# A two-layer retention and latent-attention trunk: the later modulation summed along rows, loaded early, and a reordered first unit

## The chip, the cores and the metric

The kernel runs on one core of one Trainium2 chip. The metric is device time in microseconds (us) for one call; lower is better. The engines are named as in the profile: PE (TensorE, matmuls; PEld are its weight loads), DVE (VectorE), ACT (ScalarE), POOL (GpSimd) and SP (SyncE, which only issues DMA transfers here). Each takes its instructions in order.

## What is computed

One sequence of 512 tokens, width 2048, float32, two layers. Each layer is normalised, shifted, scaled and gated by a conditioning vector `c`:

```python
c_act = jax.nn.silu(c)
for i in range(DEPTH):
    mod = (c_act @ ada_w[i] + ada_b[i])[:, None, :]          # 2048 -> 3 * 2048
    shift, scale, gate = jnp.split(mod, 3, axis=-1)
    h = rmsnorm(x, norm_g[i]) * (1.0 + scale) + shift
    y = retention_branch(...) if i == 0 else mla_branch(...)
    x = x + gate * y
return rmsnorm(x, final_norm_g)
```

Layer 1 (`i == 0`) is multi-scale retention with 8 heads: an input projection to queries and keys (256 each per head), values and a gate (512 each per head), chunked retention, a group norm, a SiLU gate and an output projection. Layer 2 is latent attention with 16 heads, again with a SiLU gate. The modulation is a vector times a 2048 x 6144 matrix per layer, some 100 MB of weights in all that are used once.

## The kernel before

Every large product is made in three matmuls (`mm3`), of a high and a low half of each operand, so every weight tile that arrives is cast on ACT (high half) and subtracted on DVE (low half) before PE reads it. PSUM has four banks under the tag `acc` and four under `aux`. SBUF tiles are taken from tagged pools: a tag has a fixed number of buffers, and a new tile waits until the oldest holder of a buffer is done, with a store's landing if a store reads it. Those that matter here are `tmp` (6 buffers of 128 x 512), `whi` and `wlo` (3 each, halves of weights), `raw` (3, weights as they arrive), and in the pool `lp`, which lives while layer 1 is projected, `st` (2), `bw` (2) and `bm` (2).

The program goes in stages. (1) The first unit and the seven that follow it compute head 0's projections (value, gate, query-key) for two contraction tiles of 128 at a time, while x is normalised and transposed (`transpose`) and while the first layer's shift and scale arrive from `ada_t`, a copy of the weights with outputs on rows. `load_mod` loads 128 outputs x 2048, `sum_mod` multiplies them on DVE with c, which stands on every partition (`c_all`), and sums along the row in the same instruction (L358); `make_first` makes one contraction tile of h from it (hT), its low half on DVE. `swap` saves partial sums from four banks on ACT and puts back others. (2) Heads 1 to 7: for heads 1 to 5 eight query-key steps of 24 matmuls, then for every head sixteen steps for values and gate together (`heads_steps`, `seven_steps`), the second eight of 18 matmuls. At a head's end `finish` evacuates the banks x_ (values) and s_ (gate) on ACT through `keep_rows`, adds y_ to the tiles m4 and m5 on DVE, and stores all eight row blocks to DRAM on POOL's queue. m4 and m5 are `tmp` tiles that were filled from banks some steps earlier. (3) The query-key steps of heads 6 and 7, and the output projection of layer 1 beside the retention of all heads. (4) Layer 2, with its gate projections (`g2_steps`), the attention and the last projection.

What is left of the modulation, first-layer gate and all of layer 2, is spread over stages 2 to 4 in eight pieces of 1024 outputs (`later_modulation`). A piece has 16 loads of 512 KB from `ada_w`, with the contraction on partitions. DVE multiplies each by one column of silu(c) per partition and adds it into `am` (L893, L895); two steps later PE sums `am` over partitions with a column of ones into eight columns of an `aux` bank (`sum_modulation`, L907), and `use_modulation` adds the biases. `rows` of a step says how many loads are issued at the end of the step before it; their adds come in that step, behind the preparation of the next step's weights. Four pieces are loaded in stage 2 (one load a step in the query-key steps of heads 2 to 5, and in second halves), two in stage 3 (`light`), two in stage 4 at two loads a step. `behind` and `queued` fix the order on an engine: what they enclose is put behind the last instruction so far on the engines named.

`keep_rows` takes its staging tile from `st`, or from another function if it is given one (`own`): the gate's tiles and every second query-key tile come from `tmp`.

Of the kernel before, what the change touches and what calls it, by code (L numbers as in the profile page):

```python
# [16 lines left out]
P = 128  # L17
# [32 lines left out]
def hybrid_trunk_kernel(  # L50
# [39 lines left out]
    x1_d = dram.tile([D, T], F32, name="x1_d")  # L90
    sg2_d = dram.tile([D, T], F32, name="sg2_d")
# [120 lines left out]
    cact = base.tile([P, KD], F32, name="cact")  # L212
    ACT.dma_start(cact, c.rearrange("o (p k) -> p (o k)", p=P))
    ACT.dma_start(rt, rot_c)
    ACT.activation(cact, cact, AF.Silu)
# [84 lines left out]
    ada0 = ada_w[0].rearrange("(p k) n -> p k n", p=P)  # L300
    ada1 = ada_w[1].rearrange("(p k) n -> p k n", p=P)

# [38 lines left out]
    def load_mod(kt, s):  # L341

        aw = l0p.tile([P, D], F32, tag="aw", bufs=4, name=f"aw_{kt}_{s}")
        n = 2 if kt == 0 else 1
        for j in range(n):
            cols = slice(j * D // n, (j + 1) * D // n)
            nc.sync.dma_start(aw[:, cols], ada_t[s * D + kt * P : s * D + (kt + 1) * P, cols])
        return aw
# [114 lines left out]

    ss = [small(f"x_ss_{t}", 2) for t in range(NT)]
# [26 lines left out]
    queued(diagonal, NT - 1)  # L491
    low_v = queued(prepares["v", 0])
# [15 lines left out]
    for kt in range(6):  # L508
        queued(queued(transpose, kt))
    def load_unit(u):  # L510
# [8 lines left out]
    late = {}  # L519

    def prepare_ahead(u, first=None):
# [5 lines left out]
        if first is not None:  # L527
            queued(first)
# [6 lines left out]
        late[u] = queued(prepares[there, u])  # L535
# [3 lines left out]
    def prepare_behind(u):  # L539

        low = queued(make_first, 2 * u + 1)
        queued(late[u])
        return low

# [7 lines left out]
    lows = [queued(prepares[kind, 0]) for kind in ("g", "qk")]  # L552
    for low in lows:
        queued(low)
# [99 lines left out]
    class Step:  # L654
# [3 lines left out]
        def __init__(self, load=None, prepare=None, multiply=None, follow=None, rows=0, sums=None, banks_free=False):  # L658
            self.units = [(load, prepare)] if load else []
            self.multiply, self.follow = multiply, follow or (lambda: None)  # L660
            self.rows, self.sums, self.banks_free = rows, sums, banks_free
# [62 lines left out]
    def seven_steps(h, block, form, raw_tile, part_tiles, finish, rows, free):  # L724
# [16 lines left out]
        def step(second, u):  # L741
# [67 lines left out]
            return Step(load, prepare, multiply, follow, rows=rows(second, u), banks_free=free(second, u))  # L809
# [3 lines left out]
    def heads_steps(h):  # L813
# [3 lines left out]
        def finish(x_, s_, y_, m4, m5):  # L817
            for b in range(2):
                keep_rows(x_[b], v_d, h * T + b * P, f"v{h}_st{b}")
            for b in range(2):  # L820
                keep_rows(s_[b], g_d, h * T + b * P, f"g{h}_st{b}", AF.Silu, tmp)
# [11 lines left out]
            lambda second, u: int(second and (u % 2 == 1 or (h > 4 and u > 0))),  # L833
            lambda second, u: second and h == RH - 1 and 2 < u < 7,
# [18 lines left out]
    def in_turn(i):  # L853
        return None if i % 2 else tmp

# [5 lines left out]
    for h in range(1, RH):  # L861
        if h < 6:
# [1110 lines left out]
```

## Time and profile before

| | |
|---|---|
| median of 3 runs | 2210.42 us (2210.02 to 2212.81) |
| the profiled execution's own time | 2211.04 us |
| its span, first to last instruction | 2209.2 us, granted clock 0.996 |
| PE busy | 2171.6 us, 98% |
| DVE busy | 1569.7 us, 71% |
| ACT busy | 995.4 us, 45% |
| POOL busy | 98.4 us, 4% |
| DMA | 437.13 MB, mean 198 GB/s |

A row of a timeline is start, duration, engine, line, operation, output tile <- input tiles, shapes and count, and in brackets how long the engine had been idle and what released it. A row of waits is the waiting instruction, what released it, the total, how often, and the longest. A row of groups ends in busy time, mean nanoseconds of one, and idle time before. Matmuls overlap, so their starts and not their durations show the rate.

### The profile page before, as it was taken

The page shows a single profiled execution, that of the slowest core. Times are in us where ns is not written, and L with a number is a line of the kernel's source. Part 1 is how long each engine was busy: PE and PEld are TensorE (multiplying, and loading weights), DVE is VectorE, ACT ScalarE, POOL GpSimd, SP SyncE. Part 2 cuts the span into 40 slices and gives each one's busy share as a digit, 9 for nine tenths or more (in the row PEclk, how much of TensorE's full clock was granted, in tenths as well). Part 3 has the DMA queues.
Part 4 walks back from the last instruction along what each step waited for, and adds up shares of the span by engine and source line. Part 5 has one row for each costly group of instructions (what it writes and reads, how often), then busy time and mean ns, then how long its engine had stood idle before and what let it go on. Part 6 is the DMA issues. An engine that isn't in the chain of part 4 may idle for free.

```text
span 2209.2 us, 28064 instructions
## 1 busy us (share of the span) xinstructions
PE 2171.6 (98%) x10404; PEld 1818.8 (82%) x10404; DVE 1569.7 (71%) x2355; ACT 995.4 (45%) x1496; POOL 98.4 (4%) x175
## 2 busy tenths in 40 slices
PE   7999999999999999999999999999999999999997
PEld 5887888888888888888888888898888888888886
DVE  7878867677676789666776767667967677776545
ACT  5664434334343454434344445345444355554443
POOL 0010000000000000000000000010001000000000
PEclk9999999999999999999999999999999999999998
DMA  9964685867677778564646565453557623225332
GB/s 384 347 247 153 223 283 189 285 196 257 229 229 251 240 244 293 188 205 147 212 167 214 167 205 181 138 177 96 172 195 285 239 77 96 82 91 195 121 122 92
DMA packets 208207, 437.13 MB, mean 198 GB/s; under 512 B 19364, under 2 KB 64436, under 8 KB 204228
## 3 DMA queue, kind: packets, MB, share of 16 engines
q1 hardware_dynamic: 195744, 396.16, 54.1%
q0 software_dynamic: 11888, 38.90, 4.5%
q8 instruction: 81, 1.33, 0.3%
q14 instruction: 60, 0.47, 0.1%
q10 hardware_dynamic: 434, 0.28, 0.1%
HBM read 392.28 MB, written 42.99 MB: 197 GB/s over the span
## 4 chain that ended last, share of the span: by engine, by line
PE 79%; DVE 9%; ACT 5%; issue 5%; DMA 2%; POOL 0%; POOLq 0%; DVEq 0%; ACTq 0%
PE o L1192 13%; PE qk L162 4%; PE qk L160 4%; PE qk L161 4%; PE o L1892 4%; PE x L733 2%; PE x L734 2%; PE y L734 2%; PE y L732 2%; PE y L733 2%; PE x L732 2%; PE s L734 2%; PE s L733 2%; PE s L732 2%; PE g L160 2%
## 5 line engine op out<-in xcount | busy, mean ns | idle before, releaser
L1192 PE MATMUL o<-o_h,o_whi 128*128 128x512 f32 (+1 forms) x496 | 193.1, 389 | 0.0
L1192 PE MATMUL o<-o_l,o_whi 128*128 128x512 f32 (+1 forms) x496 | 192.0, 387 | 0.0
L1192 PE MATMUL o<-o_h,o_wlo 128*128 128x512 f32 (+1 forms) x496 | 191.9, 387 | 0.0
L162 PE MATMUL qk<-hT,qk_l 128*128 128x512 f32 x448 | 174.8, 390 | 0.5 <-DVE qk_l L135 0.5
L160 PE MATMUL qk<-hT,qk_h 128*128 128x512 f32 x448 | 174.8, 390 | 0.0
L161 PE MATMUL qk<-hT,qk_h 128*128 128x512 f32 x448 | 174.3, 389 | 0.0
L895 DVE SCALAR_TENSOR_TENSOR mod_am<-mod_aw,cact,mod_am 128x1024 f32<-128x1024 f32 x120 | 153.6, 1280 | 15.4 <-DMA mod_aw<-in_ada_w_dram 14.9
L135 DVE TENSOR_TENSOR o_wlo<-o_r,o_whi 128x1024 fp32r<-128x1024 f32 x61 | 74.6, 1223 | 87.2 <-ACT o_whi L134 87.2
L135 DVE TENSOR_TENSOR qk_l<-qk_r,qk_h 128x1024 fp32r<-128x1024 f32 x56 | 68.1, 1223 | 66.6 <-ACT qk_h L134 66.6
L1192 PEld LDWEIGHTS o<-o_h,o_wlo 128*128 128x128 f32 x496 | 93.6, 189 | 19.0
L1192 PEld LDWEIGHTS o<-o_l,o_whi 128*128 128x128 f32 x496 | 93.7, 189 | 18.4
L1192 PEld LDWEIGHTS o<-o_h,o_whi 128*128 128x128 f32 x496 | 93.5, 189 | 18.4
L162 PEld LDWEIGHTS qk<-hT,qk_l 128*128 128x128 f32 x448 | 84.1, 188 | 19.5 <-DVE qk_l L135 2.0
L161 PEld LDWEIGHTS qk<-hT,qk_h 128*128 128x128 f32 x448 | 84.1, 188 | 17.3
L160 PEld LDWEIGHTS qk<-hT,qk_h 128*128 128x128 f32 x448 | 84.1, 188 | 17.2
L134 ACT CAST qk_h<-qk_r 128x1024 fp32r<-128x1024 f32 x56 | 57.8, 1048 | 88.8 <-PE qk L161 68.5
L160 PE MATMUL g<-h,g_h 128*128 128x512 f32 x232 | 90.7, 391 | 0.3 <-ACT g_h L134 0.3
L161 PE MATMUL g<-h,g_h 128*128 128x512 f32 x232 | 90.3, 389 | 0.0
L162 PE MATMUL g<-h,g_l 128*128 128x512 f32 x232 | 89.8, 389 | 0.0
L358 DVE SCALAR_TENSOR_TENSOR aw<-aw,c_all 128x2048 f32<-128x2048 f32 (+1 forms) x34 | 73.3, 2160 | 2.5 <-DMA aw<-in_ada_t_dram 2.5
L134 ACT CAST o_whi<-o_r 128x1024 fp32r<-128x1024 f32 x61 | 63.5, 1052 | 24.1 <-PE o L1192 11.4
L135 DVE TENSOR_TENSOR o_w_lo<-o_w_raw,o_w_hi 128x1024 fp32r<-128x1024 f32 x32 | 39.0, 1220 | 34.6 <-ACT o_w_hi L134 34.5
(1249 smaller groups left out, 5983.6 us busy)
## 6 DMA issues: line engine op xcount, KB each, us to landing
mod_aw<-in_ada_w_dram SPq DMA_DIRECT2D x128, 512.0 KB, 5.4
o_r<-in_ret_w_out_dram SPq DMA_DIRECT2D x64, 512.0 KB, 4.5
aw<-in_ada_t_dram SPq DMA_DIRECT2D x30, 1024.0 KB, 8.8
qk_r<-in_ret_w_in_dram SPq DMA_DIRECT2D x112, 256.0 KB, 4.0
g_r<-in_mla_w_in_dram SPq DMA_DIRECT2D x32, 512.0 KB, 3.9
o_w_raw<-in_mla_w_out_dram SPq DMA_DIRECT2D x32, 512.0 KB, 3.9
qk_d<-qk_st POOLq DMA_DIRECT2D x32, 256.0 KB, 3.4
qk_r<-qk_d SPq DMA_DIRECT2D x32, 256.0 KB, 6.4
```

Of the source, the lines that this page charges most:

```text
L134: ACT.copy(hi, src)
L135: DVE.tensor_sub(lo, src, hi.bitcast(F32))
L160: PE.matmul(o, lhs[0], rhs[0], start=first and not seeded, stop=False, skip_group_check=seeded)
L161: PE.matmul(o, lhs[0], rhs[1], start=False, stop=False, skip_group_check=seeded)
L162: return PE.matmul(o, lhs[1], rhs[0], start=False, stop=last, skip_group_check=seeded)
L358: DVE.scalar_tensor_tensor(out=aw[:, cols], in0=aw[:, cols], scalar=1.0, in1=c_all[:, cols], op0=ALU.mult, op1=ALU.mult, accum_out=col[:, ...
L732: PE.matmul(banks[b], a[0], w[0], start=first, stop=False, skip_group_check=True)
L733: PE.matmul(banks[b], a[0], w[1], start=False, stop=False, skip_group_check=True)
L734: PE.matmul(banks[b], a[1], w[0], start=False, stop=True, skip_group_check=True)
L895: DVE.scalar_tensor_tensor(out=am, in0=aw, scalar=ck, in1=am, op0=ALU.mult, op1=ALU.add)
L1192: PE.matmul(o, w[i][:, ki, c0 + b * P : c0 + (b + 1) * P], a[j], start=first and i + j == 0, stop=last and i == 1, skip_group_check=True,)
L1892: PE.matmul(banks2[b][:, cols], w[0][i][:, 0, b * P : (b + 1) * P], o2_moving(w, u, cols)[j], start=u + i + j == 0, stop=u == KD - 1 and i ...
```

## The change

The eight later pieces are loaded from `ada_t`, which now holds both layers whole: a load is 128 outputs x 1024 contraction elements, again 512 KB, and there are again 16 a piece. DVE multiplies it by half of c on all partitions and sums along the row in one instruction. `am`, the ones matmuls on PE, `ripe`, `summed` and the markers `banks_free` go. silu(c) is written to DRAM once (`keep_c`) and read back onto all partitions, in `lp` and again in layer 2. `bw` in `lp` has three buffers; `bm` and `st` are not used there any more, and every `keep_rows` stages in `tmp`. Six of the eight pieces are loaded in stage 2, with two loads a step in the query-key steps of heads 2 to 5; the output projection of layer 1 has none; the last two stay in layer 2. In the first unit the copies of the transposes 4 and 5 come later, 6 and 7 come right after the first query-key products, the order of preparations on ACT and DVE is written out, and v is multiplied at the end for both contraction tiles with `bank_products`, after its first tile has been multiplied at the start as before.

Left out below: declarations, the parameters `free` and `banks_free` wherever they are passed, `light`, and the layout of `ada_t` on the input side.

```diff
     bias1 = l0p.tile([P, KD], F32, name="bias1")
+    def keep_c():
+        POOL.dma_start(c_d, c_all[0:1, :])
+
     ss = [small(f"x_ss_{t}", 2) for t in range(NT)]
     norm = [None] * NT
...
         if t > 0:
             queued(diagonal, t - 1)
     queued(diagonal, NT - 1)
+    keep_c()
     low_v = queued(prepares["v", 0])
     queued(lambda: DVE.tensor_scalar(out=bias1, in0=bias_c[0][:, KD:], scalar1=1.0, scalar2=None, op0=ALU.add))
...
             )
         return lambda: ACT.copy(xT[kt // 2][:, kt % 2, :], ps)
-    for kt in range(6):
+    for kt in range(4):
         queued(queued(transpose, kt))
+    copies = [queued(transpose, kt) for kt in (4, 5)]
+
     def load_unit(u):
         here, there = ("qk", "v") if u % 2 == 0 else ("v", "qk")
         load_first(here, u)
...
-    late = {}
-
-    def prepare_ahead(u, first=None):
+    late_there = {}
+
+    def prepare_ahead(u, first):
...
-        if first is not None:
-            queued(first)
+        queued(first)
...
     queued(sum_mod, 1, 0)
     queued(low)
     lows = [queued(prepares[kind, 0]) for kind in ("g", "qk")]
+    for copy in copies:
+        queued(copy)
     for low in lows:
         queued(low)
     queued(sum_mod, 1, 1)
...
     queued(swap, "v", "qk")
     low = queued(make_first, 1)
     queued(products, "qk", 0)
-    prepare_ahead(1, low)
+    for kt in (6, 7):
+        queued(queued(transpose, kt))
+    queued(sum_mod, 2, 0)
+    queued(low)
+    low = queued(prepares["v", 1])
+    queued(sum_mod, 2, 1)
+    queued(low)
     queued(products, "qk", 1)
-    queued(queued(transpose, 6))
     queued(products, "g", 1)
     queued(swap, "qk", "v")
-    low = prepare_behind(1)
-    queued(queued(transpose, 7))
-    queued(products, "v", 1)
+    low = queued(make_first, 2)
+    for s in range(2):
+        queued(sum_mod, 3, s)
+    queued(low)
+    low = queued(prepares["g", 1])
+    low3 = queued(make_first, 3)
+    queued(low)
+    late = queued(prepares["qk", 1])
+    queued(bank_products, "v", 0)
+    queued(late)
+    low = low3
     for u in range(1, NU):
         here, there = ("qk", "v") if u % 2 == 0 else ("v", "qk")
...
     lp = tc.tile_pool(name="lp", bufs=1)
     lpp = lp.__enter__()
-    def keep_rows(ps, dst_d, r0, name, func=AF.Identity, own=None):
-
-        st = lpp.tile([P, T], F32, tag="st", bufs=2, name=name) if own is None else own(name)
+    def keep_rows(ps, dst_d, r0, name, func=AF.Identity):
+
+        st = tmp(name)
         ACT.activation(st, ps, func)
         POOL.dma_start(dst_d[r0 : r0 + P, :], st)
...
             for b in range(2):
                 keep_rows(x_[b], v_d, h * T + b * P, f"v{h}_st{b}")
             for b in range(2):
-                keep_rows(s_[b], g_d, h * T + b * P, f"g{h}_st{b}", AF.Silu, tmp)
+                keep_rows(s_[b], g_d, h * T + b * P, f"g{h}_st{b}", AF.Silu)
             for b in range(2):
                 r0 = h * T + (2 + b) * P
                 DVE.tensor_add(m4[b], m4[b], y_[b])
...
         return seven_steps(
             h, lambda kt, j: wvg[kt * P : (kt + 1) * P, j, h * T : (h + 1) * T],
             lambda n, u, b: form(hT, sums1, n, u, b), *turns1, finish,
-            lambda second, u: int(second and (u % 2 == 1 or (h > 4 and u > 0))),
-            lambda second, u: second and h == RH - 1 and 2 < u < 7,
+            lambda second, u: int(second and u in ((1, 2, 3, 4, 5, 7) if h > 4 else (1, 3, 5, 7))),
         )
     sums1, sums2 = {}, {}
...
             steps += plain_steps(
                 8, 2, qk_parts_of(h), 512, f"qk{h}", acc, 4,
                 lambda w, ki, kt, b: w_block(w, ki, b), lambda w, ki, kt, b: act_row(hT[kt]),
-                lambda b, ps, h=h: keep_rows(ps, qk_d, (4 * h + b) * P, f"qk{h}_st{b}", own=in_turn(b)),
-                rows=lambda u, h=h: int(h > 1),
+                lambda b, ps, h=h: keep_rows(ps, qk_d, (4 * h + b) * P, f"qk{h}_st{b}"),
+                rows=lambda u, h=h: 2 * int(h > 1),
                 sums=lambda u, h=h: {0: 2, 1: 3, 3: 4, 4: 5, 6: 6, 7: 7}.get(u) if h == 1 else None,
-                banks_free=lambda u: u < 5,
             )
         steps += heads_steps(h)
-
-    ripe, summed, clock = [], [], [0]
-
-    def later_modulation(pool, pieces, tags=("bm", (("bw", 2),))):
-
+    def later_modulation(pieces, silu_c, buffers):
+
+        n = 0
         for i, sect, part in pieces:
             name = f"mod_{i}_{sect}_{part}"
-            c0 = sect * D + part * 1024
-            am = pool.tile([P, 2, T], F32, tag=tags[0], bufs=2, name=f"{name}_am")
-            for k in range(KD):
-                tag, bufs = tags[1][k % len(tags[1])]
-                aw = pool.tile([P, 2, T], F32, tag=tag, bufs=bufs, name=f"{name}_aw{k}")
-                nc.sync.dma_start(
-                    aw, (ada0, ada1)[i][:, k : k + 1, c0 : c0 + 1024].rearrange("p k (a n) -> p (k a) n", a=2)
-                )
-
-                def add(aw=aw, am=am, k=k, what=(name, i, sect, part, am)):
-                    ck = cact[:, k : k + 1]
-                    if k == 0:
-                        DVE.tensor_scalar(out=am, in0=aw, scalar1=ck, scalar2=None, op0=ALU.mult)
-                    else:
-                        DVE.scalar_tensor_tensor(out=am, in0=aw, scalar=ck, in1=am, op0=ALU.mult, op1=ALU.add)
-                    if k == KD - 1:
-                        ripe.append((clock[0], what))
-
-                yield add
-
-    def sum_modulation(age=2):
-
-        while ripe and clock[0] - ripe[0][0] >= age:
-            name, i, sect, part, am = ripe.pop(0)[1]
-            ps = aux(f"{name}_ps")
+            mc = base.tile([P, 2, 8], F32, tag="mod_c", bufs=2, name=f"{name}_c")
             for b in range(8):
-                PE.matmul(ps[:, b : b + 1], am[:, b // 4, b % 4 * P : (b % 4 + 1) * P], crow, start=True, stop=True)
-            summed.append((i, sect, part, ps[:, 0:8]))
-
-    def use_modulation():
-        while summed:
-            i, sect, part, mc = summed.pop(0)
-            if sect == 2:
-                cols = slice(part * 8, part * 8 + 8)
-                DVE.tensor_add(gate_c[i][:, cols], mc, gate_bias[i][:, cols])
-            else:
-                modulate(i, mc if sect == 0 else None, mc if sect == 1 else None, part * 8, 8)
+                for j in range(2):
+                    pool, tag, bufs = buffers[n % len(buffers)]
+                    n += 1
+                    aw = pool.tile([P, 2, T], F32, tag=tag, bufs=bufs, name=f"{name}_{b}{j}")
+                    r0 = sect * D + (8 * part + b) * P
+                    nc.sync.dma_start(
+                        aw, ada_t[i, r0 : r0 + P, j * 1024 : (j + 1) * 1024].rearrange("p (a n) -> p a n", a=2)
+                    )
+
+                    def add(aw=aw, j=j, b=b, mc=mc, i=i, sect=sect, part=part):
+                        DVE.scalar_tensor_tensor(
+                            out=aw, in0=aw, scalar=1.0, in1=silu_c[j], op0=ALU.mult, op1=ALU.mult,
+                            accum_out=mc[:, j, b : b + 1],
+                        )
+                        if b == 7 and j == 1:
+                            use_modulation(i, sect, part, mc)
+
+                    yield add
+
+    def use_modulation(i, sect, part, mc):
+        both = small(f"mod_{i}_{sect}_{part}_s", 8)
+        DVE.tensor_add(both, mc[:, 0, :], mc[:, 1, :])
+        if sect == 2:
+            cols = slice(part * 8, part * 8 + 8)
+            DVE.tensor_add(gate_c[i][:, cols], both, gate_bias[i][:, cols])
+        else:
+            modulate(i, both if sect == 0 else None, both if sect == 1 else None, part * 8, 8)
     def token_sums(ps, ss, n0, n):
...
             lambda w, ki, kt, b: w_block(w, ki, b), lambda w, ki, kt, b: act_row(hT[kt]),
             lambda b, ps, h=h: keep_rows(
                 ps, qk_d, (4 * h + b) * P, f"qk{h}_st{b}",
-                own=tmp,
             ),
         )
     n_p = len(steps)
-    light(block, ())
     steps += block
     heads = [retention(0, k4), retention(1, k4, odd)]
...
         for r, after in zip(cols, [*cols[1:], None]):
             block += round_steps(n, r, go_on(n, r, after))
         heads += [retention(2 * n + 2 + i, big) for i in range(2)]
-        light(block, (0, 2, 3, 4, 6, 7, 10, 11, 12, 14, 15))
         steps += block
...
         g23[i + 1].beside["form"].append(lambda n=n: latent_scale(n))
         g23[2 + 2 * i].beside["multiply"].append(lambda n=n: latent_transposes(n))
         g23[3 + 2 * i].beside["form"].append(lambda n=n, g_c=g_c: latent_parts(n, g_c))
-    for step in g23[8:]:
-        step.banks_free = True
     steps += g23
     def all_rows():
-        yield from later_modulation(lpp, [(i, s_, n) for i, s_ in ((0, 2), (1, 0)) for n in range(2)])
-        while "l1" not in pools:
-            yield None
-        yield from later_modulation(pools["l1"], [(1, 1, n) for n in range(2)], ("odd1", (("odd0", 2),)))
+        c_all = lpp.tile([P, 2, 2, T], F32, name="c_all_p")
+        nc.sync.dma_start(c_all.rearrange("p a b n -> p (a b n)"), c_d.rearrange("o n -> (o n)").partition_broadcast(P))
+        pieces = [(i, s_, n) for i, s_ in ((0, 2), (1, 0), (1, 1)) for n in range(2)]
+        yield from later_modulation(pieces, [c_all[:, j] for j in range(2)], [(lpp, "bw", 3)])
         while "l2" not in pools:
             yield None
-        yield from later_modulation(pools["l2"], [(1, 2, n) for n in range(2)], ("bm", (("bw", 2), ("pt", 4))))
+        silu_c = [k4b(f"c_{j}", F32) for j in range(2)]
+        for j, half in enumerate(silu_c):
+            nc.sync.dma_start(
+                half.rearrange("p a n -> p (a n)"),
+                c_d[0:1, j * 1024 : (j + 1) * 1024].rearrange("o n -> (o n)").partition_broadcast(P),
+            )
+        yield from later_modulation(
+            [(1, 2, n) for n in range(2)], silu_c, [(pools["l2"], "bw", 2), (pools["l2"], "pt", 4), (pools["l2"], "pt", 4)]
+        )
     later = all_rows()
     loads = [load for step in steps for load, _ in step.units]
...
     n_loaded = 3
     n_prepared = prepare_for(0)
     for b in range(4):
-        queued(keep_rows, qk0[b], qk_d, b * P, f"qk0_st{b}", AF.Identity, in_turn(b))
+        queued(keep_rows, qk0[b], qk_d, b * P, f"qk0_st{b}")
     for b in range(3):
-        queued(keep_rows, g0[b], g_d, b * P, f"g0_st{b}", AF.Silu, tmp)
+        queued(keep_rows, g0[b], g_d, b * P, f"g0_st{b}", AF.Silu)
     for i, step in enumerate(steps):
-        clock[0] = i
         if i == n_p:
             lp.__exit__(None, None, None)
             l1 = tc.tile_pool(name="l1", bufs=1)
             pools["l1"] = l1.__enter__()
         if i == n_l2:
-            assert not ripe and not summed
             l1.__exit__(None, None, None)
             l2 = tc.tile_pool(name="l2", bufs=1)
             pools["l2"] = l2.__enter__()
...
                 load()
         n_prepared += prepare_for(i + 1)
         with behind(V_, A_):
-            use_modulation()
             for form_ in step.beside["form"]:
                 form_()
-        with behind(T_):
-            if step.banks_free:
-                sum_modulation()
         with behind(T_):
             step.multiply()
         with behind(T_):
```

More of the change, by code (lines that the diff above doesn't have):

```diff
@@ L534, in prepare_ahead @@
         low = queued(prepares["g", u])
-        late[u] = queued(prepares[there, u])
+        late_there[u] = queued(prepares[there, u])
         queued(low)
@@ L541, in prepare_behind @@
         low = queued(make_first, 2 * u + 1)
-        queued(late[u])
+        queued(late_there[u])
         return low
@@ L722, in turns, with seven_steps @@
         return raw_tile, part_tiles
-    def seven_steps(h, block, form, raw_tile, part_tiles, finish, rows, free):
+    def seven_steps(h, block, form, raw_tile, part_tiles, finish, rows):
         x_, s_, y_, z_, m1, m4, m5 = ([None] * 2 for _ in range(7))
@@ L807, in follow @@
                     finish(x_, s_, y_, m4, m5)
-            return Step(load, prepare, multiply, follow, rows=rows(second, u), banks_free=free(second, u))
+            return Step(load, prepare, multiply, follow, rows=rows(second, u))
         return [step(second, u) for second in (False, True) for u in range(KD // 2)]
@@ L1099, in place @@
                 block[first + i].beside[kind].append(fn)
-    def light(block, which):
-        for i in which:
-            block[i].rows = 1
-        for i in (2, 3):
-            block[i].banks_free = True
     block = []
```

21 lines of the change are left out of this document (6 added, 15 removed).

## The prediction

> **What bounds the kernel now.** The page comes first.
>
> ```profile
> span 2209.2 us, 28064 instructions
> PE 2171.6 (98%) x10404; PEld 1818.8 (82%) x10404; DVE 1569.7 (71%) x2355; ACT 995.4 (45%) x1496; POOL 98.4 (4%) x175
> PE   7999999999999999999999999999999999999997
> ```
>
> TensorE is busy in every slice but the first and the last, and everything else has room on average. So two things can move the time: TensorE instructions that go or come, and a wait that makes TensorE stop. I then asked for the waits of TensorE alone, to see how many stops there are to win back.
>
> ```profile
> PE c_ps L427 <- DMA c_all<-in_c_dram: 6.1, 1, 6.1
> PE xT_ps L501 <- ACT xT L506: 3.2, 1, 3.2
> ```
>
> Both are in the first 45 us. Between the layer 1 projections, where the change puts most of its loads, the answer names no wait of as much as a microsecond. There the kernel can only lose, unless work goes. The profiled execution took 2211.04 us, its span 2209.2; the median of the runs is 2210.42, 0.6 less. I sum against 2211.04 and take 0.6 off at the end. 0.2% is 4.4 us, about what a measurement of this kernel can tell from no change.
>
> **TensorE's sums go.** Each of the eight later pieces ends in one group of matmuls with a column of ones.
>
> ```profile
> 418.38 0.39 PE L160 MATMUL qk<-hT,qk_h 128*128 128x512 f32 x1
> ...
> 419.75 1.84 PE L907 MATMUL mod_ps<-ones,mod_am 128*128 128x1 f32 x16
> 421.45 0.49 PE L160 MATMUL qk<-hT,qk_h 128*128 128x512 f32 x1
> 421.77 0.40 PE L161 MATMUL qk<-hT,qk_h 128*128 128x512 f32 x1
> ```
>
> Six ordinary matmuls start between 418.38 and 419.75, so they are 0.228 us apart; a step of 24 takes 5.45 us. The group holds the next one back from 419.75 to 421.45, 1.70 us, and the one after starts 0.32 later instead of 0.23: 1.8 us. 8 x 1.8 = 14.4 us, all on the path. One group costs more:
>
> ```profile
> 1392.57 1.95 PE L907 MATMUL mod_ps<-ones,mod_am 128*128 128x1 f32 x16 [0.26 <-DVE o_l L1075]
> 1394.89 0.63 PE L1192 MATMUL o<-o_l,o_whi 128*128 128x512 f32 x1
> 1395.32 0.63 PE L1192 MATMUL o<-o_h,o_wlo 128*128 128x512 f32 x1
> 1390.00:1400.00 10.00, 9.74 (x53) 8.24 (x52) 5.68 (x11) 3.36 (x5) 0.00 (x0) 0.83 0.23 79
> ```
>
> Behind it matmuls start 0.43 apart and the granted clock of these 10 us is 0.83, 10 x 0.17 = 1.7 us lost, and 0.26 was idle: -2.0 if the slow stretch goes with the group, 0 if transposes alone cause it. I take -2.0, since only here a stop lay between transposes and the group. The Trainium skill ("TensorE: Matmul & The Clock Gate", Part 1) lets the clock halve only after an idle window of about 3.4 us; no such gap stands before 1394, so the trace does not agree, and by the rule this term would be 0.
>
> **VectorE's adds.** As many loads and adds as before, 128 of 512 KB, in another layout.
>
> ```profile
> L895 DVE SCALAR_TENSOR_TENSOR mod_am<-mod_aw,cact,mod_am 128x1024 f32<-128x1024 f32 x120 | 153.6, 1280 | 15.4 <-DMA mod_aw<-in_ada_w_dram 14.9
> L358 DVE SCALAR_TENSOR_TENSOR aw<-aw,c_all 128x1024 f32<-128x1024 f32 x4 | 4.7, 1219 | 0.0
> L358 DVE DVE_READ_ACCUMULATOR aw<-aw,c_all 128x1 f32 x5 | 0.4, 82 | 0.0
> ```
>
> A row with its sum costs 1.219 + 0.082 = 1.30 us against 1.28: nothing, as VectorE is at 71%.
>
> **The evacuations get one pool of buffers.** This is the term I fear. At a head's end `finish` keeps four tiles: two of v, two of the gate. Before, v goes to `st`, the gate to `tmp`. Afterwards all four want `tmp`, which has six buffers, and m4 and m5 hold four of them until the end. So v takes the last two, and the gate's evacuation must wait until a store of v has landed. Head 1, ScalarE, then GpSimd, then TensorE:
>
> ```profile
> 292.78 1.28 ACT L615 ACTIVATE g_st<-s 128x512 f32<-128x512 f32 x2
> 296.66 0.63 ACT L827 ACTIVATE m<-m 128x512 f32<-128x512 f32 x1 [0.56 <-DVE m L826]
> 297.20 1.99 ACT L134 CAST qk_h<-qk_r 128x1024 fp32r<-128x1024 f32 x2
> 292.32 1.22 POOL L616 DMA_DIRECT2D v_d<-v_st  x2 [70.94 <-ACT v_st L615]
> 294.62 0.39 PE L160 MATMUL qk<-hT,qk_h 128*128 128x512 f32 x1
> L616 POOL DMA_DIRECT2D v_d<-v_st x8: 539/539/556, 292.3 to 653.9; - x8
> DMA to landing us min/median/max: 4.9/6.2/6.8
> ```
>
> The last two rows are the v stores of heads 1 to 4. The second store of a pair is the later; I take the middle of the upper half, 6.5. It starts 0.68 after the first (293.0), lands at 299.5, and the second gate tile leaves its bank 0.64 later, 300.1. Queued behind on ScalarE are the two SiLUs of m (0.63 each, 301.4) and then the cast of the next step's weights (1.0, 302.4), which starts at 297.20 now. TensorE wants those weights after one step of 24 matmuls, 294.62 + 5.45 = 300.07: 2.3 us late. VectorE's low half (a subtraction of 1.23) is wanted by the third matmul, 0.45 after the first, so 0.8 more: 3.1 us. The gate's banks themselves are wanted by the third group of 6, at 297.35; the first store of a pair lands in about 5.4 (middle of the lower half), so the bank is free at 292.32 + 5.4 + 0.64 = 298.4, 1.05 late, which is part of the 3.1. Four heads: 12.4 us. Behind heads 5 and 6 another head follows at once, which wants the gate's banks after 6 matmuls instead of 12:
>
> ```profile
> 776.15 1.07 POOL L616 DMA_DIRECT2D v_d<-v_st  x2 [73.65 <-ACT v_st L615]
> 778.40 0.39 PE L732 MATMUL s<-vg_00e_h,sums 128*128 128x512 f32 x1
> DMA to landing us min/median/max: 4.4/4.9/5.4
> L616 POOL DMA_DIRECT2D v_d<-v_st x2: 539/539/539, 852.8 to 853.3; - x2
> DMA to landing us min/median/max: 5.7/6.4/7.2
> L616 POOL DMA_DIRECT2D v_d<-v_st x2: 539/539/539, 931.6 to 932.3; - x2
> DMA to landing us min/median/max: 4.0/4.1/4.1
> ```
>
> Head 5: 776.15 + 4.4 + 0.6 = 781.15, wanted at 778.40: 2.75 late; the second, 776.7 + 5.4 + 0.6 = 782.7, wanted 0.68 after the first, adds 0.85; 0.4 for the next cast: 4.0. Head 6: landings 1.3 and 1.8 later, 5.3. Head 7 is as head 1 with 4.1 for 6.5: 3.1 - 2.4 = 0.7. Sum 12.4 + 4.0 + 5.3 + 0.7 = +22.4 us. Bounds: 0, if stores land as the gate rows' do below, to 30, if the extra loads of a step delay each store by 1 us more. That ScalarE does stand still for a landing, with the cast queued behind it, is seen where four gate rows of layer 2 share three buffers:
>
> ```profile
> 1537.68 0.60 ACT L1433 ACTIVATE sgs<-g 128x512 f32<-128x512 f32 x1 [1.79 <-DMA sg_d<-sgs]
> 1538.18 1.04 ACT L134 CAST g_h<-g_r 128x1024 fp32r<-128x1024 f32 x1
> DMA to landing us min/median/max: 2.3/2.7/5.2
> ```
>
> **Two rows a step, three buffers.** In the query-key steps of heads 2 to 5 two rows are loaded a step instead of one.
>
> ```profile
> 294.60:335.00 40.40, 40.40 (x180) 33.43 (x179) 23.29 (x24) 11.12 (x12) 2.44 (x5) 1.00 0.82 294
> 1650.00:1765.00 115.00, 115.00 (x544) 96.40 (x543) 79.08 (x86) 46.73 (x75) 7.83 (x10) 1.00 0.76 268
> mod_aw<-in_ada_w_dram SPq DMA_DIRECT2D x128, 512.0 KB, 5.4
> ```
>
> The columns are busy times, then clock, DMA share and GB/s. 294 GB/s are 0.82 of the DMA engines, so about 359 are all of them. Eight more rows of 0.52 MB in 40.4 us add 104: 398, or 40.4 x 398/359 = 44.8 us, 4.4 too long, 17.6 over four blocks. That is the upper bound. The lower is 0: weights are asked for three units ahead, and VectorE needs 1.23 + 2 x 1.30 = 3.8 of a step's 5.45 us. Layer 2 runs two rows a step at 268 GB/s without a stop, but with six buffers. With three, a buffer comes round in 5.4 + 1.3 + 0.1 = 6.8 us, two rows each 4.5. I take +4. The rows taken out of the output projection relieve it of nothing that TensorE waits for: 0. The copy of c over all partitions is one load of twice a row's bytes, which holds the first row's add once: 0 to 3 against the 5.4 of a row, taken 0.5.
>
> **The first unit.** T6 and T7 move ahead, and v's first contraction tile is multiplied twice: 12 matmuls, +2.7 us.
>
> ```profile
> 42.64 1.99 PE L501 MATMUL xT_ps<-x_diag,x 128*128 128x128 f32 x8 [3.18 <-ACT xT L506]
> 47.49 2.29 DVE L358 SCALAR_TENSOR_TENSOR aw<-aw,c_all 128x2048 f32<-128x2048 f32 x1 [0.29 <-DMA aw<-in_ada_t_dram]
> 49.71 0.69 DVE L248 TENSOR_TENSOR hT<-h_3f,hT 128x512 fp32r<-128x512 f32 x1
> ```
>
> The 3.18 us stop before T7 goes, and the doubled matmuls fill it. But hT_3's low half now stands behind more subtractions on VectorE, still after the sum whose rows land about 47.5, so the second unit's v ends where it does now. Net 0, bounds -3.2 and +2.7. `keep_c` is one store on GpSimd's queue, an engine at 4%, before its first evacuation store: 0.
>
> **Sum.** -14.4 - 2.0 + 22.4 + 4 + 0.5 + 0 = +10.5; 2211.04 + 10.5 - 0.6 = 2221 us.
>
> **Rivals.** *Stores land early.* If the v stores land in about 2.7 us, as the last fence before the row loads shows for layer 2, the gate's bank is free at 292.32 + 2.7 + 0.64 = 295.7, before 297.35, and the 22.4 goes: -11.9, 2198.5, faster. For it: the same size and queue. Against: every v store in these heads took 4.0 or more, with DMA at 0.8 instead. The Trainium skill ("DMA: Bandwidth & Descriptors", Anatomy of one DMA) gives such a store 2.0 us plus its bytes at 436 GB/s, an estimate of 2.6 us for 256 KB; the busy stretches here do not agree. *Casts go ahead.* If the instruction order puts the next cast before the waiting gate tile, only the bank waits are left: 4 x 1.05 + 3.6 + 4.9 = 12.7 (heads 5 and 6 without 0.4 each), so +0.8, 2211, no change. *Row loads saturate the queues* in the four blocks, the full 17.6 instead of 4: 2235. The point is where three buffers come round slower than 8.2 us, a landing of 6.8. *The sum along rows is dearer*: excluded by its 1.30 us.
>
> **How the numbers follow.** Forecast 0.52, early stores 0.18, casts ahead 0.12, saturated 0.18. The forecast's own range is 2209 to 2234. Faster: early stores and a tail, 0.20; within 0.2% (2206 to 2214.8): casts ahead and the forecast's low edge, 0.17; slower 0.63. The range 2202 to 2238 leaves out most of the early stores and the worst of the saturation.
>
> **What would show it.** No mod_ps group, and TensorE's count down by 128 less 12, to about 10288. ScalarE waiting for the landing of v stores, seven times, and TensorE for s banks or for the next cast, about 20 us together. DMA share near 1 in the blocks of heads 2 to 5. If TensorE shows no new waits between 290 and 940 us, the forecast is wrong and the kernel is faster.

## The result, and the profile after

The changed kernel takes 2230.02 us (median, 2228.68 to 2233.83) against 2210.22 (2208.81 to 2212.81) for the kernel before: ratio 1.009, interval 1.0077 to 1.0103, slower by 0.9%. In the medians that is +19.8 us. The profiled execution took 2228.71 us, and its span is 17.7 us longer than before; the account below goes by it. The sum of the prediction said +10.5.

The page's engine row and the waits of TensorE alone (waiting instruction, releaser, total us, times, longest):

```profile
span 2226.9 us, 28018 instructions
PE 2172.2 (98%) x10288; PEld 1809.9 (81%) x10288; DVE 1570.4 (71%) x2491; ACT 995.7 (45%) x1496; POOL 99.3 (4%) x176
```

```profile
PE qk L161 <- ACT g_st L631: 10.6, 4, 2.9
PE s L748 <- ACT g_st L631: 5.8, 4, 2.9
...
PE v L396 <- DVE hT L246: 3.0, 2, 2.1
```

10288 matmuls, as expected, and a new wait at the top: the gate's banks, 16.4 us, where before named no wait of a microsecond in this stage. The chain behind it at head 1, in the timeline of ScalarE:

```profile
302.65 0.60 ACT L631 ACTIVATE g_st<-s 128x512 f32<-128x512 f32 x1 [6.99 <-DMA v_d<-v_st]
303.44 0.60 ACT L631 ACTIVATE g_st<-s 128x512 f32<-128x512 f32 x1 [0.19 <-DMA v_d<-v_st]
303.93 1.14 ACT L843 ACTIVATE m<-m 128x512 f32<-128x512 f32 x2
304.97 1.98 ACT L135 CAST qk_h<-qk_r 128x1024 fp32r<-128x1024 f32 x2
```

ScalarE stands still for 6.99 us until a store of v has landed; the two SiLUs and the cast of the next weights are queued behind. Over the whole run (the tile's answer, idle time ahead of the gate's evacuation and what ended it):

```profile
  DMA v_d<-v_st: 43.3, 13
```

The ones matmuls are gone, and each took 1.85 us with it: matmul by matmul against before, the lag falls by 1.85 at every place where a group stood. At the end of stage 2 (before's 1003 us) the lag (how much later the same matmul starts than before) is 27.0; from there it falls to 17.8 at the last matmul.

### The profile page after: what moved, and what is told of

Same layout as the page of the kernel before. It is cut to its first block, busy times and chain, and to the rows that moved or that the text cites. A ratio compares the mean times of both kernels' runs of the same rounds, so it can differ in the third digit from the quotient of the medians.

```text
span 2226.9 us, 28018 instructions
## 1 busy us (share of the span) xinstructions
PE 2172.2 (98%) x10288; PEld 1809.9 (81%) x10288; DVE 1570.4 (71%) x2491; ACT 995.7 (45%) x1496; POOL 99.3 (4%) x176
## 4 chain that ended last, share of the span: by engine, by line
PE 45%; issue 39%; DVE 7%; ACT 5%; DMA 2%; POOL 2%; POOLq 0%; DVEq 0%; SPq 0%; ACTq 0%
PE o L1184 13%; PE o L1880 4%; PE g L161 2%; PE g L162 2%; PE g L163 2%; PE o L163 1%; PE o L162 1%; PE o L161 1%; PE qk L396 1%; PE qk L163 1%; PE qk L161 1%; PE qk L162 1%; ACT p L1703 1%; PE pT L1716 1%; PE v L396 1%
## 5 line engine op out<-in xcount | busy, mean ns | idle before, releaser
L161 PE MATMUL qk<-hT,qk_h 128*128 128x512 f32 x448 | 177.1, 395 | 10.6 <-ACT g_st L631 10.6
L136 DVE TENSOR_TENSOR o_wlo<-o_r,o_whi 128x1024 fp32r<-128x1024 f32 x61 | 74.5, 1223 | 111.7 <-ACT o_whi L135 111.7
L902 DVE SCALAR_TENSOR_TENSOR mod<-mod,c_all_p 128x1024 f32<-128x1024 f32 x96 | 116.6, 1222 | 30.4 <-DMA mod<-in_ada_t_dram 30.1
L136 DVE TENSOR_TENSOR qk_l<-qk_r,qk_h 128x1024 fp32r<-128x1024 f32 x56 | 68.1, 1223 | 59.4 <-ACT qk_h L135 59.4
L161 PEld LDWEIGHTS qk<-hT,qk_h 128*128 128x128 f32 x448 | 85.3, 190 | 30.0 <-ACT g_st L631 12.3
L162 PEld LDWEIGHTS qk<-hT,qk_h 128*128 128x128 f32 x448 | 85.3, 190 | 17.7
L135 ACT CAST qk_h<-qk_r 128x1024 fp32r<-128x1024 f32 x56 | 57.8, 1049 | 85.5 <-DMA qk_r<-in_ret_w_in_dram 27.7
L136 DVE TENSOR_TENSOR o_w_lo<-o_w_raw,o_w_hi 128x1024 fp32r<-128x1024 f32 x32 | 39.0, 1220 | 34.6 <-ACT o_w_hi L135 34.5
```

The source lines that it names most:

```text
L135: ACT.copy(hi, src)
L136: DVE.tensor_sub(lo, src, hi.bitcast(F32))
L161: PE.matmul(o, lhs[0], rhs[0], start=first and not seeded, stop=False, skip_group_check=seeded)
L162: PE.matmul(o, lhs[0], rhs[1], start=False, stop=False, skip_group_check=seeded)
L902: DVE.scalar_tensor_tensor(out=aw, in0=aw, scalar=1.0, in1=silu_c[j], op0=ALU.mult, op1=ALU.mult, accum_out=mc[:, j, b : b + 1],)
```

## Experiments

Where a lag or a distance of starts is given, the two traces were laid against each other matmul by matmul, the ones matmuls left out.

**e1: the staging alone.**

```diff
-        st = lpp.tile([P, T], F32, tag="st", bufs=2, name=name) if own is None else own(name)
+        st = tmp(name)
```

> The kernel before with one edit: every keep_rows stages in tmp. Ones matmuls, loads and first unit are as before. Theory (the gate's banks wait for the landing of v's stores because tmp has two buffers left): TensorE stops at the s banks behind heads 1 to 6, about 1.4 us plus some 1.5 us of slow matmuls behind heads 1 to 4 (store landings stay at 4.9 to 6.8 us, since no load is added) and 4 to 5.5 us behind heads 5 and 6, together 18 to 24 us: 2228 to 2234 us. Rival (the stops come only with the extra row loads, which delay the stores): under 5 us, 2210 to 2215 us. Rival (the next weights' casts behind the waiting ACT instruction set the length, not the bank): 22 us as well, but TensorE's waits name the halves of the weights and not the s banks.

2231.5 us against 2209.65, ratio 1.0096 (1.0082 to 1.0109): +21.9. Waits of TensorE:

```profile
PE s L732 <- ACT g_st L615: 6.8, 3, 3.6
...
PE qk L160 <- ACT g_st L615: 4.5, 4, 1.7
...
PE qk L162 <- DVE qk_l L135: 2.0, 4, 0.5
```

Head 1, ScalarE and then TensorE:

```profile
298.60 0.60 ACT L615 ACTIVATE g_st<-s 128x512 f32<-128x512 f32 x1 [4.99 <-DMA v_d<-v_st]
300.95 0.60 ACT L615 ACTIVATE g_st<-s 128x512 f32<-128x512 f32 x1 [1.75 <-DMA v_d<-v_st]
301.44 1.14 ACT L827 ACTIVATE m<-m 128x512 f32<-128x512 f32 x2
302.48 2.93 ACT L134 CAST qk_h<-qk_r 128x1024 fp32r<-128x1024 f32 x3
```

```profile
304.83 0.50 PE L162 MATMUL qk<-hT,qk_l 128*128 128x512 f32 x1 [0.53 <-DVE qk_l L135]
```

This is the predicted chain link by link, the last one the low half of the next weights. The row-load rival falls: no load was added here. The casts' rival falls too: the banks take 11.3 us of these waits, the halves of the weights 2.0. By the lags the seven head ends cost 3.5, 2.0, 3.3, 1.8, 4.7, 5.4 and 0.4.

**e2: the row sums alone.** `later_modulation` as in the change, c in the places of `bm`, `odd1` and `k4b`; `st`, `bw` with two buffers, the number of loads a step and the first unit as before.

> The kernel before with the new layout of the modulation alone: rows of ada_t summed on DVE, c kept and read back on all partitions (in the place of the bm buffers, of odd1, of k4b), no mod_ps on TensorE; st, the number of loads in each step, two bw buffers and the first unit stay as before. Theory (the row sums are pure gain, the loss comes from the buffers): minus 14.4 for the eight groups, minus 2.0 for the slow stretch at 1392 to 1398, plus 0 to 1 for reading c: 2193 to 2197 us. Rival (a sum along rows with its accumulator read costs the path through DVE): above 2200 us, with TensorE waiting for low halves that DVE makes.

2202.9 us, ratio 0.9965 (0.9953 to 0.9978): -6.8, not -15 to -16. Both theories missed: the eight groups give their 1.85 each and the slow stretch at 1394 is gone, but in between the lag grows in every run of seven-product steps, in layer 2's (zc, xc, yc) too, where no row is loaded. There matmuls start 229.1 ns apart on average, in before 226.67; in the query-key steps, with a row load each, they stay at 226.67. e1 and e3 have 226.67 throughout, the changed kernel 229.1. So it comes with the row sums, but not from their work.

**e3: the first unit's order alone** (the lines of the change from the copies of T4 and T5 to `bank_products`).

> The kernel before with the new order of the first unit alone (later copies of T4 and T5, T6 and T7 ahead, v's first tile multiplied twice). The prediction's step said 0 (bounds minus 3.2 and plus 2.7). The trace of after stands 2.8 us behind at 75 to 164 us: by it plus 2.3 to 2.8, 2212.5 to 2213.2 us. Rival (the 2.8 is made up later, when the evacuation of head 0 finds its buffers free): 2210 us.

2214.9 us, ratio 1.002 (1.0011 to 1.0029): +5.2, above the 2212.5 to 2213.2 expected, though the interval reaches down to it. The lag behind the first unit is 4.2 and stays; 1.5 more comes at the last group of ones matmuls, from a slow stretch that is no part of the first unit. The changed kernel has 2.9 at 70 us and 2.3 behind head 0. VectorE, changed kernel:

```profile
49.27 1.22 DVE L332 TENSOR_TENSOR qk_wlo<-qk_raw,qk_whi 128x1024 fp32r<-128x1024 f32 x1 [1.66 <-ACT qk_whi L330]
50.41 2.28 DVE L353 SCALAR_TENSOR_TENSOR aw<-aw,c_all 128x2048 f32<-128x2048 f32 x1
...
52.62 0.68 DVE L246 TENSOR_TENSOR hT<-h_3f,hT 128x512 fp32r<-128x512 f32 x1
```

The sum that before started at 47.49, when its rows had landed, now waits for the subtraction ahead of it. That subtraction stood ahead of it before too, but there its cast was made early (41.06 us). Now the cast stands on ScalarE behind the copies of `swap` and the two activations of hT_3 and starts at 48.20:

```profile
47.50 0.80 ACT L245 ACTIVATE h_3f<-xT,b_col,a_col 128x512 f32<-128x512 f32 x1
48.20 1.98 ACT L330 CAST qk_whi<-qk_raw 128x1024 fp32r<-128x1024 f32 x2
```

So hT_3's low half starts at 52.62 instead of 49.71, and TensorE waits 2.1 us for it (L396 above). e3 has a second wait of 2.2 us a little later, the query-key products behind a copy of `swap`; in the changed kernel it is 0.6. Why it differs stays open; e7 and e8 below have 2.2 there as well.

**e4: e1 and e2 together.**

> Both of the edits before together: row sums in before's schedule of loads, and every keep_rows in tmp. If the two parts add up and nothing else matters: e1 + e2 - before, about 2212 to 2218 us, and what is left to the changed kernel (2230) is the extra loads of two a step and the first unit: 12 to 18 us. Rival (the extra loads cost nothing): about 2227 us, the changed kernel less the first unit's 2.8.

2228.4 us, ratio 1.0082 (1.0068 to 1.0095), where the two alone add up to 2224.8. With one row load a step it has a lag of 27.7 at the end of stage 2, the changed kernel with two has 27.0. That looks as if the extra loads cost nothing, but the two lose in different places. The table has the lag gained across the heads' ends, with 1.85 added back for each group passed and the lag of e11 (below) taken off where the addresses differ, and beside it the landings of v's stores at heads 1 to 4:

| | heads 1 to 4, us | heads 5 to 7, us | v's landings, middle |
|---|---|---|---|
| prediction, staging alone | 12.4 | 10.0 | 6.2 (before) |
| e1, staging alone | 10.6 | 10.5 | 6.4 |
| e4, with row sums, one load a step | 14.6 | 14.9 | 6.6 |
| changed kernel, two loads a step | 17.6 | 9.8 | 7.2 |

e4, the v stores of heads 1 to 4:

```profile
L616 POOL DMA_DIRECT2D v_d<-v_st x8: 539/539/548, 293.7 to 666.8; - x8
DMA to landing us min/median/max: 5.8/6.6/7.4
```

Behind heads 1 to 4, where the steps with two loads begin, the changed kernel loses about 3 us more than e4 (e7 and e8 below lose 17.0 and 17.7, e10 20.4), and v's stores land later. Behind heads 5 and 6 e4 loses more; there its schedule has one row load more in each head. No run changes the number of loads alone, so these 3 us are read from a comparison and not shown by an experiment.

**e5 to e7: addresses.** Removing `cact` (64 bytes a partition) and adding `mod_c` (128) moves tiles in SBUF. In the allocation of the built programs the large base tiles start at 96 modulo 256 in before and the tiles of the stage pools also at 96; in e2 and the changed kernel at 32 and 160.

```diff
e5, e7:
+    pad = base.tile([P, 16], F32, name="pad")
     vcol = base.tile([P, P + 56], F32, name="vcol")
e6:
-    cact = base.tile([P, KD], F32, name="cact")
...
+    cact, _ = (base.tile([P, KD], F32, tag="late", bufs=2, name=f"late{n}") for n in range(2))
+    queued(ACT.activation, cact, c_raw, AF.Silu)
```

> The row sums of e2 with 64 unused bytes a partition in the place of cact, so that every large tile has the address that it has in the kernel before (96 modulo 256, where e2 has 32). In e2 the seven-product steps (heads 1 to 7, layer 2's latent) start their matmuls 229.1 ns apart and in before 226.67, with and without row loads, which takes back 7.0 of 16.8 us. Theory (where the tiles lie in SBUF sets this): the steps are back at 226.7 ns, 7.0 us less than e2: 2195 to 2197 us. Rival (the row sums on DVE or their loads slow TensorE's reads): 229 ns stay, 2203 us.

> The kernel before with its modulation, loads and buffers, but with the addresses of e2: cact is allocated behind the other tiles (large tiles 64 bytes lower, the layer 1 pool 64 higher); its silu moves to the end of the first unit. Theory (addresses): the seven-product steps at 229.1 ns, plus 7 us: 2216 to 2218 us. Rival (row sums): 226.67 ns stay, 2210 us.

> The changed kernel with 64 unused bytes in the place of cact. Theory (addresses): minus 6 to 7, 2223 to 2224 us. Rival (row sums): no change, 2230 us.

e6, 2216.9 us, ratio 1.0028 (1.0017 to 1.0039), has 229.1 ns without any row sum. So it is the addresses. But e5 stays at 2203.0 with 229.1 ns, and e7 is no faster either (2232.6): the base tiles are back at 96 there, and that is not what counts. The pool tiles lie at 224 in both. That e7 is 2.6 us slower than the changed kernel goes with its first unit: its lag behind head 0 is 5.5 instead of 2.3.

**e8: TensorE kept busy inside the stop.**

```diff
+                    if u == 0 and ki == 0 and b == 2 and name in ("qk2", "qk3", "qk4", "qk5"):
+                        busy = aux(f"{name}_busy")
+                        for n_ in range(14):
+                            PE.matmul(busy, w["hl"][0][:, 0, 0:P], hT[0][:, 0, :], start=True, stop=True)
```

> The changed kernel with 14 matmuls more (3.2 us, into a free bank, never read) ahead of the third group of the first query-key step of heads 2 to 5, that is inside the stop for the gate's bank, so that TensorE does not stand still while it waits. The four stops of after (2.94, 3.06, 2.62, 2.65 us) are followed by matmuls 0.43 us apart, and each head's end costs 3.8 to 5.0 in all, 18.2 together. Theory (the stop itself brings the slow matmuls): the four ends cost 4 x 3.2 = 12.8, so minus 5: 2224 to 2226 us, and no start-to-start distance of 0.43 behind them. Rival (the slow matmuls come from what runs beside them, the other evacuations and casts): 0.43 stays, 2230 to 2232 us.

In the changed kernel's timeline the four stops are 2.78, 2.90, 2.46 and 2.49 us long. Behind the third, at 553.33 us, the rate is full at once, which the expectation overlooked; behind the other three come slow matmuls, 0.43 us apart. The first (columns of the second fence: window, its length, TensorE's busy time and count, granted clock, DMA share, GB/s):

```profile
303.30 0.80 PE L161 MATMUL qk<-hT,qk_h 128*128 128x512 f32 x1 [2.78 <-ACT g_st L631]
...
304.32 0.63 PE L163 MATMUL qk<-hT,qk_l 128*128 128x512 f32 x1
304.75 0.63 PE L161 MATMUL qk<-hT,qk_h 128*128 128x512 f32 x1
```

```profile
303.30:306.90 3.60, 3.60 (x9) 0.53 0.78 300
306.90:310.00 3.10, 3.10 (x15) 1.00 0.67 215
```

e8:

```profile
302.96 3.34 PE L709 MATMUL qk_busy<-hT,qk_h 128*128 128x512 f32 x14
306.14 0.40 PE L161 MATMUL qk<-hT,qk_h 128*128 128x512 f32 x1
306.38 0.39 PE L162 MATMUL qk<-hT,qk_h 128*128 128x512 f32 x1
...
310.25 0.50 PE L163 MATMUL qk<-hT,qk_l 128*128 128x512 f32 x1 [0.53 <-DVE qk_l L136]
```

Behind none of the four stands a slow matmul now, so the stops bring them, if not every time. But 2230.8 us is no gain, and neither are the heads' ends: behind heads 1 to 4 e8 loses 17.7 us and the changed kernel 17.6. TensorE now waits 0.5 us at each for the low half of the next weights (L136), which stands behind ScalarE's cast, and v's stores land in 7.5 us in the middle instead of 7.2. Right on the cause, wrong on the price: that the chain of casts ends at nearly the same time and hides the slow clock is the likely reason, but no run separates it from the later landings.

**e9 to e12: the distance.** 128 unused bytes (64 in e12) behind the base tiles move the stage pools alone.

```diff
+    late_pad = base.tile([P, 32], F32, name="late_pad")
     lp = tc.tile_pool(name="lp", bufs=1)
```

> The row sums of e2 with 128 unused bytes behind the base tiles, so that the tiles of the stage pools (layer 1's projections, its output projection, layer 2) move up by 128. In before, base tiles and pool tiles lie at the same address modulo 256 (96 and 96); in e2 at 32 and 160, in e5 at 96 and 224, in e6 at 32 and 160, and these three have 229.1 ns in the seven-product steps. Here 32 and 32. Theory (the distance between base tiles and pool tiles modulo 256 decides): 226.7 ns, 7.0 us less than e2: 2195 to 2197 us, below both kernels. Rival (the pool's own address must be 96 modulo 256): 229 ns stay, 2203 us. Second rival (the row sums themselves, beside a layout effect in e6): 2203 us too, but then e11 has 226.7 or 229 on its own.

> The changed kernel with the same 128 unused bytes, addresses 32 and 32. Theory (distance): minus 7, 2223 us, with the stops at the heads' ends and the first unit's 2.3 us left. Rivals: 2230 us.

> The kernel before with 128 unused bytes behind the base tiles and nothing else: base tiles stay at 96, pool tiles go to 224 modulo 256. Theory (distance): 229.1 ns in the seven-product steps, plus 7, 2216 to 2217 us. Rival (the row sums, or the moved base tiles of e6): 226.67 ns, 2210 us.

> The same with 64 bytes: 96 and 160 modulo 256, a distance of 64. Which distances count is not known: if any distance other than 0 does, plus 7, 2217 us; if only 128 does, 2210 us; something between if the cost goes with the overlap.

| | base, pools modulo 256 | starts apart, layer 2's seven-product steps | median us | ratio to before |
|---|---|---|---|---|
| e9 row sums | 32, 32 | 226.7 ns | 2197.2 | 0.9943 (0.9931 to 0.9956) |
| e10 changed kernel | 32, 32 | 226.7 | 2227.9 | 1.0084 (1.007 to 1.0098) |
| e11 before | 96, 224 | 229.2 | 2215.3 | 1.0026 (1.0015 to 1.0036) |
| e12 before | 96, 160 | 229.9 | 2216.5 | 1.0031 (1.0019 to 1.0043) |

The distance decides, and any of the two tried costs about the same. e9 beats both kernels, by 12.7 us. Which matmuls pay is seen in e11, TensorE, starts in the first column, some in a row left out:

```profile
226.98 0.40 PE L735 MATMUL z<-vg_01o_h,hT 128*128 128x512 f32 x1
...
229.77 0.39 PE L735 MATMUL x<-vg_02e_h,hT 128*128 128x512 f32 x1
...
258.62 0.39 PE L735 MATMUL y<-vg_07o_h,sums 128*128 128x512 f32 x1
...
259.98 0.40 PE L735 MATMUL s<-vg_07e_h,sums 128*128 128x512 f32 x1
...
261.37 0.40 PE L735 MATMUL z<-vg_07o_h,hT 128*128 128x512 f32 x1
```

Before, the first two of these places:

```profile
226.62 0.39 PE L732 MATMUL z<-vg_01o_h,hT 128*128 128x512 f32 x1
...
229.34 0.39 PE L732 MATMUL x<-vg_02e_h,hT 128*128 128x512 f32 x1
```

`part_tiles` takes every fourth pair of weight halves from the pool, which are the o halves of odd steps, and the last four tiles of sums, read in steps 6 and 7, lie in the pool too. From z of step 1 to x of step 2 there are 12 matmuls with weights in the pool and activations in the base: 2.79 us, 0.2325 each, before 2.72, 0.2267. In step 7, y has both operands in the pool: 6 matmuls in 1.36, 0.2267, full rate. s has its weights in the base and its sums in the pool: 1.39, 0.232.

e10 got back 2.1 us of the 6 that its distances give: its waits for the gate's banks, 12.3 and 7.1 us, are 3.0 longer than the 10.6 and 5.8 of the changed kernel. v's stores at heads 1 to 4 landed in 7.6 us in the middle there, 7.2 in the changed kernel. Why stays open; e7 and e8 have 7.2 and 7.5.

## Why the prediction came out as it did

By lag, against the profile of before: the eight groups -14.8 (8 x 1.85), the slow stretch -2.0, the heads' ends and the loads +27.0, the addresses +6.0 (5.15 in stage 2 and 0.85 in layer 2, from e11), the first unit +2.3. Together +18.5, measured +17.8. So the forecast of a slower kernel came true by the wait that it named, and most of what it fell short by is one term that is not in its sum, the addresses. That the time still lies in the range is its width. The 27.0 is a difference: the lag at the end of stage 2, which happens to be 27.0 too, plus the 7.4 that four groups had given back by then, less 5.15 and 2.3; head by head, as in the table at e4, it is 27.4.

- **Sums on TensorE, -14.4:** right, 14.8. **Slow stretch, -2.0:** it went, 2.1 by lag. But it also went in e1, e6 and e11, which keep the group and a stop of 0.25 us ahead of it. e11:

```profile
1397.66 1.95 PE L910 MATMUL mod_ps<-ones,mod_am 128*128 128x1 f32 x16 [0.25 <-DVE o_l L1078]
1399.47 0.49 PE L1195 MATMUL o<-o_h,o_whi 128*128 128x512 f32 x1
1399.79 0.40 PE L1195 MATMUL o<-o_l,o_whi 128*128 128x512 f32 x1
1400.03 0.40 PE L1195 MATMUL o<-o_h,o_wlo 128*128 128x512 f32 x1
```

In e1 and e3 a slow stretch follows the last group instead or as well, with no stop ahead. So the stop that the prediction reasoned from does not decide. Of the six profiles that have the groups four show such a stretch behind the sixth or the last one, of the eight without groups none at these places. The groups have a part in it; what decides stays open, and the -2.0 was in part luck.
- **Evacuations, +22.4, and row loads, +4:** right in sum, 26.9 with c's 0.5 against 27.0, and that it is so near is in part luck, as the shares moved. e1 measures the first alone at 21.1 (the seven head ends, predicted 12.4 + 4.0 + 5.3 + 0.7; head 6's own two landings, 1.3 and 1.8 later than head 5's, give 5.8 by the same steps). The loads took another path than the +4 was taken for, which was a weight or a row that comes late inside the four blocks. The share of the DMA engines did go to nearly 1 there, as two of the changed kernel's windows of the four blocks show (window, length, busy time of TensorE, its loads, VectorE, ScalarE and GpSimd, then clock, DMA share and GB/s),

```profile
307.00:345.00 38.00, 38.00 (x169) 31.43 (x168) 30.65 (x45) 8.91 (x10) 0.73 (x2) 1.00 0.97 339
432.00:470.00 38.00, 38.00 (x167) 31.35 (x167) 30.10 (x45) 8.76 (x11) 1.08 (x2) 0.99 0.94 332
```

but TensorE has 38.00 us busy of 38.00: VectorE waited for the rows, and TensorE for nothing. What the loads seem to cost is about 3 us at the ends of heads 1 to 4, by v's stores that land later (the table at e4); the prediction had this only in its upper bound of 30. The other part of the 27.0 is that heads 1 to 4 cost 4.0 more when row sums and staging meet, with one load a step (e4 against e1). Why stays open.
- **VectorE's adds, 0:** right, a row takes 1.222 + 0.08 us, and e9 shows no loss but 2.3 us behind heads 5 and 6, where TensorE waits for low halves.
- **First unit, 0:** wrong, +2.3 in the changed kernel and some 4 in e3. The step "the second unit's v ends where it does now" failed: it took the sum as bound by its rows alone and overlooked the subtraction ahead of it, which now waits 1.66 us for a cast that has moved back on ScalarE. The bound of +2.7 held for the changed kernel, not for e3.
- **Addresses:** not in the sum at all, +6.0, the largest miss. That a column vector of 64 bytes goes and 128 bytes come was in the declarations of the diff; that this moves every large tile, and that TensorE feels it, was not asked.
- **Rivals:** *early stores* fell, v's stores took 7.2 us in the middle (7.0 to 7.5) at heads 1 to 4; *casts go ahead* fell, the casts stand behind the waiting evacuation; *saturated queues* fell for TensorE, though the share was reached: in the two windows above the rows landed in 5.6 and 5.7 us in the middle, under the 6.8 that it named. The waits that were to show it came: the gate's evacuation behind v's landing, at the heads named.

```profile
L632 POOL DMA_DIRECT2D v_d<-v_st x8: 539/539/548, 295.3 to 670.4; - x8
...
DMA to landing us min/median/max: 7.0/7.2/7.5
```

## What to carry to other kernels

When a pool of staging buffers runs out, the next evacuation waits for the landing of a store: count the buffers that are free at the moment of the evacuation, and name what is queued behind it on that engine. After any change of declarations, compare the addresses of the two operands of each matmul, and the start-to-start distance in a stage that the change does not touch; padding of 128 bytes was worth 5.7 us here (e2 to e9). And cut a mixed change into its parts before judging it: the staging, which loses 21.9 (e1), hid row sums that gain 6.8 as they stand (e2) and 12.7 with the padding (e9).

## What the runs showed of the hardware

- A matmul of 128x512 whose two operands start at different addresses modulo 256 (64 or 128 apart) took 0.2325 us from start to start instead of 0.2267, 2.6% more; with both shifted alike it took 0.2267. The Trainium skill ("SBUF — State Buffer", Operand start alignment) asks only that an operand starts at a multiple of its element size; all of these did. Whether other distances cost, whether 256 is the period, and why the distance costs, was not tried.
- The granted clock fell to 0.53 for 3.6 us behind a stop of 2.78 us, and with 14 matmuls in the place of such stops it stayed at 1.00 (e8). The Trainium skill ("TensorE: Matmul & The Clock Gate", Part 1) has the clock halve after an idle window of about 3.4 us; these stops were shorter. The length alone does not decide: behind the heads' ends a stop of 1.82 us was followed by slow matmuls (e4, clock 0.56 for 3.9 us), and stops of 2.46 us (changed kernel) and 3.07 us (e10) by full rate:

```profile
549.11 0.50 PE L161 MATMUL qk<-hT,qk_h 128*128 128x512 f32 x1 [1.82 <-ACT g_st L615]
...
549.81 0.63 PE L163 MATMUL qk<-hT,qk_l 128*128 128x512 f32 x1
550.24 0.63 PE L161 MATMUL qk<-hT,qk_h 128*128 128x512 f32 x1
```

```profile
427.27 0.50 PE L161 MATMUL qk<-hT,qk_h 128*128 128x512 f32 x1 [3.07 <-ACT g_st L634]
427.61 0.39 PE L162 MATMUL qk<-hT,qk_h 128*128 128x512 f32 x1
427.84 0.40 PE L163 MATMUL qk<-hT,qk_l 128*128 128x512 f32 x1
```

- Two stores of 256 KB on the same queue, some 8 us apart, differ by more than two times: at head 1 of the changed kernel v's landed in 7.3 and 7.4 us, the gate's behind them in about 3.0. The windows (GpSimd's busy time, clock, DMA share, GB/s) have

```profile
296.00:303.00 7.00, 1.03 (x2) 1.00 0.93 316
303.50:306.50 3.00, 2.45 (x5) 0.50 0.73 281
```

so the slow landings go with the busier stretch: 0.93 of the DMA engines were busy under the first, 0.73 under the second. No run changes the load alone.
